# Rearranged transitions into and out of two FFN stages: one modulation vector moved to TensorE, other product order, other groups, a new cost in the order planner

## The chip, the cores and the metric

The kernel runs on one core of a Trainium2 chip. The metric is the device time of one execution in microseconds, as the median of several runs. The engines that matter here are TensorE (PE in the profile; its weight loads are PEld), VectorE (DVE), ScalarE (ACT), GpSimd (POOL) and the DMA queues, of which SyncE (SP) issues nearly all loads of weights. The engines run side by side, each through its own queue in order, and wait for one another through semaphores.

## The reference

Two layers of a generator block on 512 latent tokens and 256 context tokens of width 1024. The last layer doesn't update the context.

```python
for l in range(DEPTH):                                   # DEPTH = 2
    mod  = c_act  @ w_mod[l] + b_mod[l]                  # six vectors sh1 sc1 g1 sh2 sc2 g2 for the latents
    modc = cc_act @ w_mod[l] + b_mod[l]                  # and six for the context
    px = (rmsnorm(x, norm1_g[l]) * (1.0 + sc1) + sh1) @ w_in[l] + b_in[l]
    ...                                                  # three head groups: mLSTM, gated MLP, convolution -> y_x
    x = x + g1 * (y_x @ w_out[l])
    x = x + g2 * swiglu(rmsnorm(x, norm2_g[l]) * (1.0 + sc2) + sh2, w_gu[l], w_down[l])
    ...                                                  # the same for the context, if not the last layer
return rmsnorm(x, final_g)

def swiglu(h, w_gu, w_down):
    gate, up = split(h @ w_gu, 2)                        # hidden width 2816 = 22 tiles of 128
    return (silu(gate) * up) @ w_down
```

The modulation vectors are numbered 0 to 5 in the order above: vector 5 of layer 0 is g2, the gate of its FFN; vector 1 of layer 1 is sc1, which the first norm of layer 1 needs.

## The kernel before

**Numbers.** All matrix products are of float32 data, each operand being split into a rounded part `hi` and a rest `lo`; a product is three matmuls (hi·hi, hi·lo, lo·hi: lines 528 to 530 in the plain products, 1887 to 1889 in the paired ones). Weights arrive in `raw` buffers (four of 512 KB); ACT copies them to `hi` (L374, L457) and DVE subtracts to get `lo` (L376, L334). The split buffers (`spl`, four) hold a whole plain weight tile each or, in the FFN's paired part, are cut into eight units.

**The order.** The program is written as many small generators ("threads") that ask for an engine with a cost, for an event or for a buffer. A planner (`Plan.run`) plays them against each other with these costs, always taking the request that can start earliest, then by priority (a lower number first), and in doing so emits every engine's instructions. So the costs in `PE(n)`, `DVE2(n)`, `ACT(n)` decide in which order each in-order queue holds its work; they do nothing at run time. A main list `steps` sets PE's order and `ORDER` follows it for the weights' loads. `spread(a, b)` mixes list b evenly into list a.

**Modulation vectors.** A vector can be made in two ways. `mod_steps` does it on PE: eight steps, each of four matmuls (L650) that read a raw weight buffer and free it. `modh_steps` does it on DVE: eight loads of 512 KB, and per load two or four multiply-adds (L724 the first, L727 the others), four where both token kinds need the vector; each half ends with a few matmuls on PE (L737). Before, vectors 2, 3, 4 of layer 0 are made on PE in its first stage, vector 5 of layer 0 and vector 1 of layer 1 on DVE in the second half of that stage (32 DVE instructions each), and vectors 0, 2, 3, 4, 5 of layer 1 on DVE during layer 0's FFN.

**The FFN.** Its first tiles of hidden units (`NPLAIN`, two per layer) are computed plainly: gate and up columns of eight contraction steps over all tokens. Each further tile j is a "pair": gate and up column together form a 2 x 2 block product, done with seven products instead of eight, each over half of the contraction (four steps of three matmuls) and half of the tokens (384 in layer 0, 256 in layer 1). Weight sums are made by DVE in the raw buffers (L420); the sums of the activations, the "T-forms", are made once per layer: L1781 to L1790 on DVE, L1794 the copy on ACT, L1796 the rest on DVE, for k = 0 to 3. The products s1, s2, s3 and a22 need a form, step k the form of k; a11, a12 and s4 read the activations directly. In PSUM bank A collects a11, s2, s3, a22 in turn, and `copy_out` copies A after a11, s2 and s3 (`x`, `x`, `d`, L1958); d gets C added (L1962) before s4 goes into C; bank B holds a12. `pair_out` then makes the hidden tile from x, d, A, B and C. Order in a pair before: a11, then a22 and s4 of the pair before, then s1, s2, a12, s3.

The down projection runs in groups of hidden tiles (`FFN_GROUPS`: start and count). A group's eight columns times two token halves are mixed into the pairs' steps after its tiles are there (`D_BLOCKS`); each half's result is added to `xT` by DVE (L2023). The last group comes after the last pair, followed by the next norm (squares L778, sums L781, `stat` L831, the power on POOL L264, `rstdb` L846, then L893, L868, L870).

Of the kernel before, what the change touches and what calls it, by code (L numbers as in the profile page):

```python
# [31 lines left out]
RV_BV, RV_BVS, RV_BGT, RV_LG, RV_LB = 0, 512, 768, 784, 1040  # L32
NRV = 1296
WB_Q, WB_K, WB_O, WB_U, WB_A, WB_G = 0, 4, 8, 12, 14, 16
FFN_GROUPS = (((0, 4), (4, 4), (8, 4), (12, 4), (16, 3), (19, 3)), ((0, 6), (6, 6), (12, 5), (17, 5)))
NPLAIN = (2, 2)
D_BLOCKS = (2, 4)
PAIR = ("a11", "a22", "s4", "s1", "s2", "a12", "s3")
GV_SLABS = ((0, 3), (3, 3), (6, 2))


# [133 lines left out]


def PE(n, passes=1):
    return ("e", "pe", max(107.0, n / 2.4) * passes)


def MM(n):
# [42 lines left out]
def backbone(ctx, tc, xT_d, cT_d, wmod_d, wb_d, wgv_d, wv_d, wout_d, wgu_d, wd_d, sw_d, sb_d, cv_d, rv_d, id_d, mk_d, out_d):  # L224
    nc = tc.nc
    pe, dve, act, pool, sp = nc.tensor, nc.vector, nc.scalar, nc.gpsimd, nc.sync
# [46 lines left out]
    def ev(*key):  # L273
        if key not in EV:
            EV[key] = Event()
        return EV[key]
# [27 lines left out]
    def loader():  # L304
        for i, key in enumerate(ORDER):
            if key[0] == "x":
                yield DMA(P * T * 8)
                sp.dma_start(out=xT[:, key[1]:key[1] + 2, :], in_=xT_d[:, key[1]:key[1] + 2, :])
                fire(ev("x", key[1]), DMA_LAT)
                continue  # L310
            if key[0] == "gp":
                if key[3] == PAIR[0]:
                    RAW[key[:3]] = rs = []
                    for up in range(2):
                        yield A("raw")
                        r = buf("raw", [P, KD, P], "raw")
                        yield DMA(P * KD * P * 4)
                        sp.dma_start(out=r.rearrange("p a b -> p (a b)"), in_=wgu_d[key[1], 2 * key[2] + up])
                        rs.append(r)
                        fire(ev("raw", key[:3], up), DMA_LAT)  # L320
                continue
            src, a, b = wsrc(key)
            tag = "slot" if key[0] == "modq" else "raw"
            yield A(tag)
            r = buf(tag, [P, a, b], "raw")
            RAW[i] = r
            yield DMA(P * a * b * 4)
            sp.dma_start(out=r if key[0][:3] == "mod" else r.rearrange("p a b -> p (a b)"), in_=src)
            fire(ev("raw", i), DMA_LAT)
# [130 lines left out]
    def splitter():  # L460
        in_units = set()
        for i, key in enumerate(ORDER):
            if key[0] == "x":
                continue
            if key[0] == "gp":
                if key[1] not in in_units:
                    in_units.add(key[1])
                    spawn(to_units(), 6)
                yield A("un")
                SPL[i] = UN.pop(0)  # L470
                fire(ev("u", i))
                if key[3] == PAIR[0]:
                    spawn(pair_sums(key[:3]), 0)
                continue
            if key[0] == "d":
                if key[2] < len(FFN_GROUPS[key[1]]) - 1:
                    m = (wsrc(key)[1] + 3) // 4
                    yield A("un", m)
                    spawn(split_units(i, key, [UN.pop(0) for _ in range(m)]), 0)
                    continue  # L480
                if key[1] in in_units:
                    in_units.remove(key[1])
                    spawn(from_units(), 6)
            if key[0][:3] == "mod":
                spawn(as_is(i), 0)
                continue
            yield A("spl")
            spawn(split(i, key), 0)
# [424 lines left out]
    def spread(a, b):  # L913
        out, j = [], 0
        for i, x in enumerate(a):
            out.append(x)
            while j < len(b) and j * len(a) < (i + 1) * len(b):
                out.append(b[j])
                j += 1
        return out  # L920

    def layer(l):
        last = l == L - 1
# [12 lines left out]
        def E(*key):  # L936
            return ev(l, *key)
# [9 lines left out]
        steps = []  # L947
# [728 lines left out]
        mid = None  # L1676
        if l == 0:
            mid = True
        steps += tiles([k_col(h) for h in range(H)], GB, GA, KD, hsrc, hwait, wide=True, mid=mid, ahead=AHEAD[0])
        first = len(steps)  # L1680
# [7 lines left out]
        if not last:  # L1688
            steps = steps[:first] + spread(steps[first:], [m for v in (2, 3, 4) for m in mod_steps(l, v)])
# [16 lines left out]
        def out_col(d):  # L1706
            def evac(p, grp):
                yield from resid(l, 2, p, d, grp, lambda g: norm(l, 1, g))
            return (("o", l, d), evac, 0.5)

        def spawn_gs(m, which):
            def fn():
                spawn(norm_gs(m, which))
                return
                yield
            return ([], fn)

        steps.append(spawn_gs(l, 1))
        steps += tiles([out_col(d) for d in range(KD)], gl, gg, KD, hsrc, lambda k, g: E("ys", g["t0"], k), YK, wide=True, ahead=AHEAD[1])


        hid, gups = {}, {}
# [3 lines left out]
        fg = FFN_GROUPS[l]  # L1726
# [97 lines left out]
        def gu_col(i):  # L1824
            j, up = divmod(i, 2)

            def evac(p, g):
                if up:
                    yield from gu_evac(j, g, gups.pop((j, g["t0"])), p)
                else:  # L1830
                    gups[j, g["t0"]] = p
            return (("gu", l, i), evac, 0.6)
# [59 lines left out]
        def pair_steps(j, before):  # L1892
            key = ("gp", l, j)
            q = pr[j] = {}

            def first(w):
                yield A("ps")
                q["A"] = ps("bA")
                yield from product(q["A"], w, (0, 0), True)
                spawn(copy_out(j, 0), 0.6)  # L1900

            def fifth(w):
                yield A("ps")
                q["C"] = ps("bC")
                yield from product(q["C"], w, 0, True)

            def sixth(w):
                yield W(E("cp", j, 0))
                yield from product(q["A"], w, 3, False)
                spawn(copy_out(j, 1), 0.6)  # L1910

            def second(w):
                yield A("ps")
                q["B"] = ps("bB")
                yield from product(q["B"], w, (1, 0), True)
                spawn(join_one(j), 0.6)

            def seventh(w):
                yield W(E("cp", j, 1))
                yield from product(q["A"], w, 1, False)  # L1920
                spawn(copy_out(j, 2), 0.6)

            out = [([key + ("a11",)], first)]
            if before is not None:
                out += pair_end(before)
            return out + [([key + ("s1",)], fifth), ([key + ("s2",)], sixth), ([key + ("a12",)], second), ([key + ("s3",)], seventh)]

        def pair_end(j):
            q = pr[j]

            def fourth(w):
                yield W(E("cp", j, 2))
                yield from product(q["A"], w, 2, False)

            def third(w):
                yield W(E("join", j))
                yield from product(q["C"], w, (1, 1), False)
                spawn(pair_out(j), 0.5)
            return [([("gp", l, j, "a22")], fourth), ([("gp", l, j, "s4")], third)]
# [133 lines left out]
            return  # L2073
            yield

        if not last:
            early = [m for v in (5,) for m in modh_steps(l, v)] + modh_steps(l + 1, 1)
            late = first + (len(steps) - first) // 2
            steps = steps[:late] + spread(steps[late:], early)
        steps.append(([], lambda: spawn_ffn()))  # L2080
        np_ = NPLAIN[l]
        steps += tiles([gu_col(i) for i in range(2 * np_)], gl, gg, KD, hsrc, lambda k, g: ev("h", l, 1, g["t0"], k), wide=True, ahead=AHEAD[2])
        steps.append(([], plain_done))
        nfirst = len(steps)
        pairs = list(range(np_, NJ))
        blocks = [pair_steps(j, j - 1 if i else None) for i, j in enumerate(pairs)]
        for gi, (j0, nj) in enumerate(fg[:-1]):
            b0, ds = j0 + nj - np_ + 1, d_run(gi)
            nb = min(D_BLOCKS[l], len(blocks) - b0)
            for b in range(nb):  # L2090
                part = ds[b * len(ds) // nb:(b + 1) * len(ds) // nb]
                cut = 3 if blocks[b0 + b][1][0] else 1
                blocks[b0 + b] = blocks[b0 + b][:cut] + spread(blocks[b0 + b][cut:], part)
        for b in blocks:
            steps += b
        steps += pair_end(pairs[-1])
        if not last:
            steps = steps[:nfirst] + spread(steps[nfirst:], [m for v in (0, 2, 3, 4, 5) for m in modh_steps(l + 1, v, "wi")])
            steps.append(spawn_gs(l + 1, 0))
        steps.append(([], t_free))  # L2100
        steps += d_run(len(fg) - 1)
# [58 lines left out]
    for c in EARLY_LOADS + "m" * len(pkeys) + "w" * len(mkeys):  # L2160
        n = len(ORDER)
# [93 lines left out]
```

## Time and profile before

| | before |
|---|---|
| median of 3 runs | 1580.05 us (1579.65 to 1580.49) |
| profiled execution, its time | 1579.2 us |
| its span | 1577.4 us |
| mean granted PE clock | 0.982 |
| ACT busy | 678.1 us |
| weight DMA (q1) | 170.16 MB |

A span is the time from the first to the last instruction of the profiled execution. "Busy" rows of matmuls overlap, as matmuls are pipelined: the rate of PE is read from the distance between starts, not from the duration of one. A number in brackets at a row's end is the engine's idle time just before, with the instruction that ended it. "PEclk" is the share of the full clock that PE was granted.

### The profile page before, as it was taken

The numbers are of one execution on the slowest core, as the hardware profiler recorded it, in microseconds if no ns is written. First come the engines' busy times: TensorE is split into PE (matmuls) and PEld (weight loads), VectorE is DVE, ScalarE is ACT, GpSimd is POOL, SyncE is SP. The second block draws the span as 40 slices with busy tenths as digits, with TensorE's granted clock in tenths as the row PEclk, the third lists the DMA queues.
The fourth block names the chain that finished last, engine by engine and source line by source line (L and its number), as shares of the span: only waits on it lengthen the run. The fifth ranks groups of instructions, "written<-read, shape, count | busy, mean of one in ns | idle before, by whom it ended". The sixth has DMA issues, their size and how long they took to land.

```text
span 1577.4 us, 26171 instructions
## 1 busy us (share of the span) xinstructions
PE 1502.8 (95%) x10232; PEld 1398.8 (89%) x10232; DVE 1147.4 (73%) x2416; ACT 678.1 (43%) x1402; POOL 33.3 (2%) x50
## 2 busy tenths in 40 slices
PE   5999999999789999999999989999999799999997
PEld 4887888888689999999999988878999699999997
DVE  5359889777977876767777774687768876777765
ACT  4332367543433343333333343426655444444444
POOL 0000010000000000000000000000000000000000
PEclk9999999999989999999999989999999899999999
DMA  9433346543023334333334232213321223333331
GB/s 327 144 121 120 116 132 203 157 139 107 27 70 111 101 106 135 108 107 121 112 102 127 86 97 74 87 55 114 101 94 55 80 85 104 101 94 101 104 101 64
DMA packets 72824, 173.25 MB, mean 110 GB/s; under 512 B 7564, under 2 KB 20988, under 8 KB 72700
## 3 DMA queue, kind: packets, MB, share of 16 engines
q1 hardware_dynamic: 69932, 170.16, 34.1%
q8 instruction: 80, 1.31, 0.3%
q10 hardware_dynamic: 2768, 1.42, 0.3%
q14 instruction: 44, 0.36, 0.1%
HBM read 169.34 MB, written 2.21 MB: 109 GB/s over the span
## 4 chain that ended last, share of the span: by engine, by line
PE 90%; DVE 5%; DMA 2%; ACT 1%; issue 1%; POOL 0%; SPq 0%; POOLq 0%; DVEq 0%; ACTq 0%
PE mm L528 15%; PE mm L529 15%; PE mm L530 15%; PE bA L1887 6%; PE bA L1888 6%; PE bA L1889 6%; PE bC L1887 3%; PE bC L1888 3%; PE bC L1889 3%; PE vp L1304 2%; PE vp L1305 1%; PE vp L1306 1%; PE bB L1887 1%; PE bB L1889 1%; PE bB L1888 1%; PE stp L1441 1%
## 5 line engine op out<-in xcount | busy, mean ns | idle before, releaser
L528 PE MATMUL mm<-HH,hi 128*128 128x256 f32 (+2 forms) x1008 | 342.3, 340 | 2.9 <-ACT HH L1603 1.7
L529 PE MATMUL mm<-HH,hi 128*128 128x256 f32 (+2 forms) x1008 | 329.3, 327 | 2.6 <-DVE HH L870 2.3
L530 PE MATMUL mm<-HH,lo 128*128 128x256 f32 (+2 forms) x1008 | 329.0, 326 | 0.9 <-DVE lo L334 0.9
L374 ACT CAST hi<-raw 128x512 fp32r<-128x512 f32 (+3 forms) x368 | 214.5, 603 | 215.1 <-PE mm L529 47.5
L376 DVE TENSOR_TENSOR lo<-raw,hi 128x512 fp32r<-128x512 f32 (+3 forms) x368 | 236.7, 663 | 67.1 <-ACT hi L374 64.4
L528 PEld LDWEIGHTS mm<-HH,hi 128*128 128x128 f32 x1008 | 191.6, 190 | 24.0 <-issue 8.0
L530 PEld LDWEIGHTS mm<-HH,lo 128*128 128x128 f32 x1008 | 191.4, 190 | 16.2 <-DVE lo L334 1.3
L529 PEld LDWEIGHTS mm<-HH,hi 128*128 128x128 f32 x1008 | 191.9, 190 | 14.9 <-DVE HH L870 3.3
L530 PE MATMUL mm<-ffn,lo 128*128 128x256 f32 (+1 forms) x576 | 176.3, 306 | 2.1 <-DVE lo L376 2.1
L528 PE MATMUL mm<-ffn,hi 128*128 128x256 f32 (+1 forms) x576 | 177.1, 307 | 0.7 <-ACT ffn L2006 0.5
L529 PE MATMUL mm<-ffn,hi 128*128 128x256 f32 (+1 forms) x576 | 176.5, 306 | 0.5 <-DVE ffn L2001 0.3
L1888 PE MATMUL bA<-ffn,hi 128*128 128x384 f32 (+1 forms) x480 | 149.2, 311 | 0.0
L334 DVE TENSOR_TENSOR lo<-raw,hi 128x1024 fp32r<-128x1024 f32 (+4 forms) x90 | 99.0, 1104 | 68.2 <-ACT hi L457 62.8
L2023 DVE SCALAR_TENSOR_TENSOR xT<-mm,modc,xT 128x256 f32<-128x256 f32 (+2 forms) x208 | 95.4, 480 | 68.4 <-PE mm L530 67.2
L457 ACT CAST hi<-raw 128x1024 fp32r<-128x1024 f32 (+4 forms) x90 | 85.3, 952 | 132.2 <-PE mm L529 49.8
L420 DVE TENSOR_TENSOR raw<-raw 128x512 f32<-128x512 f32 x160 | 109.1, 686 | 19.3 <-DMA raw<-in_wgu 18.3
L1889 PE MATMUL bA<-HH,lo 128*128 128x256 f32 (+1 forms) x400 | 116.9, 292 | 0.0
L1887 PE MATMUL bA<-HH,hi 128*128 128x256 f32 (+1 forms) x400 | 116.9, 292 | 0.0
L530 PEld LDWEIGHTS mm<-ffn,lo 128*128 128x128 f32 x576 | 108.8, 189 | 2.4 <-DVE lo L376 2.4
L528 PEld LDWEIGHTS mm<-ffn,hi 128*128 128x128 f32 x576 | 108.5, 188 | 2.3 <-ACT ffn L2006 0.8
L529 PEld LDWEIGHTS mm<-ffn,hi 128*128 128x128 f32 x576 | 108.4, 188 | 1.0 <-DVE ffn L2001 0.5
L727 DVE SCALAR_TENSOR_TENSOR macc<-raw,csil,macc 128x512 f32<-128x512 f32 x140 | 102.5, 744 | 0.4
(263 smaller groups left out, 3010.2 us busy)
## 6 DMA issues: line engine op xcount, KB each, us to landing
raw<-in_wmod SPq DMA_DIRECT2D x96, 512.0 KB, 4.2
raw<-in_wgu SPq DMA_DIRECT2D x88, 512.0 KB, 4.0
raw<-in_wb SPq DMA_DIRECT2D x36, 512.0 KB, 3.6
pbt<-dr SPq DMA_DIRECT2D x40, 256.0 KB, 3.7
raw<-in_wout SPq DMA_DIRECT2D x16, 512.0 KB, 3.6
raw<-in_wd SPq DMA_DIRECT2D x32, 256.0 KB, 2.6
raw<-in_wd SPq DMA_DIRECT2D x16, 384.0 KB, 3.1
raw<-in_wd SPq DMA_DIRECT2D x16, 320.0 KB, 3.1
```

Source lines behind the costliest of these rows:

```text
L334: dve.tensor_tensor(lo, r, hi.bitcast(F32), ALU.subtract)
L374: act.copy(hi, x)
L376: dve.tensor_tensor(lo, x, hi.bitcast(F32), ALU.subtract)
L420: dve.tensor_tensor(o, x, y, op)
L528: pe.matmul(o, lhsT=hi[:, k, :], rhs=hh, start=(j == 0), stop=False)
L529: pe.matmul(o, lhsT=hi[:, k, :], rhs=hl, start=False, stop=False)
L530: pe.matmul(o, lhsT=lo[:, k, :], rhs=hh, start=False, stop=(j == nk - 1))
L727: dve.scalar_tensor_tensor(a[g], s[:, i, :], c, a[g], ALU.mult, ALU.add)
L1887: pe.matmul(o, lhsT=hi[:, k], rhs=rh, start=start and k == 0, stop=False, skip_group_check=True)
L1888: pe.matmul(o, lhsT=hi[:, k], rhs=rl, start=False, stop=False, skip_group_check=True)
L1889: pe.matmul(o, lhsT=lo[:, k], rhs=rh, start=False, stop=k == 3, skip_group_check=True)
L2023: dve.scalar_tensor_tensor(x, p[:, a - h["t0"]:b - h["t0"]], MODC[l][:, 5, d, g["g"]:g["g"] + 1], x, ALU.mult, ALU.add)
```

## The change

- `mod_steps(0, 5)`: vector 5 of layer 0 is made on PE, its eight steps spread from the middle of the out-projection (`nout`) to the end of the plain FFN columns. Vector 1 of layer 1 is made on DVE during layer 0's FFN, ahead of the others there.
- Pair order: a11, a22 and s4 of the pair before, s2, a12, s1, s3. The first pair of a layer: a11, a12, s2, s1, s3.
- `FFN_GROUPS`, layer 0: the last two groups have two and four tiles instead of three and three. `D_LAST`: the last eight steps of the last group but one come after the last pair, in both layers.
- `NPLAIN`: three plain tiles in layer 1.
- The planner's cost of a matmul: from n/2.4 to 1 + 0.455 n ns (at least 107). This lays out the order of all queues anew, over the whole kernel.

```diff
-FFN_GROUPS = (((0, 4), (4, 4), (8, 4), (12, 4), (16, 3), (19, 3)), ((0, 6), (6, 6), (12, 5), (17, 5)))
-NPLAIN = (2, 2)
+FFN_GROUPS = (((0, 4), (4, 4), (8, 4), (12, 4), (16, 2), (18, 4)), ((0, 6), (6, 6), (12, 5), (17, 5)))
+NPLAIN = (2, 3)
 D_BLOCKS = (2, 4)
-PAIR = ("a11", "a22", "s4", "s1", "s2", "a12", "s3")
+D_LAST = 8
...
 def PE(n, passes=1):
-    return ("e", "pe", max(107.0, n / 2.4) * passes)
+    return ("e", "pe", max(107.0, 1 + 0.455 * n) * passes)
...
+        nout = len(steps)
         steps += tiles([out_col(d) for d in range(KD)], gl, gg, KD, hsrc, lambda k, g: E("ys", g["t0"], k), YK, wide=True, ahead=AHEAD[1])
+        nout = (nout + len(steps)) // 2
...
             out = [([key + ("a11",)], first)]
+            mid = [([key + ("s2",)], sixth), ([key + ("a12",)], second)]
             if before is not None:
                 out += pair_end(before)
-            return out + [([key + ("s1",)], fifth), ([key + ("s2",)], sixth), ([key + ("a12",)], second), ([key + ("s3",)], seventh)]
+            else:
+                mid = mid[::-1]
+            return out + mid + [([key + ("s1",)], fifth), ([key + ("s3",)], seventh)]
...
-        if not last:
-            early = [m for v in (5,) for m in modh_steps(l, v)] + modh_steps(l + 1, 1)
-            late = first + (len(steps) - first) // 2
-            steps = steps[:late] + spread(steps[late:], early)
         steps.append(([], lambda: spawn_ffn()))
         np_ = NPLAIN[l]
         steps += tiles([gu_col(i) for i in range(2 * np_)], gl, gg, KD, hsrc, lambda k, g: ev("h", l, 1, g["t0"], k), wide=True, ahead=AHEAD[2])
+        if not last:
+            steps = steps[:nout] + spread(steps[nout:], mod_steps(0, 5))
...
             nb = min(D_BLOCKS[l], len(blocks) - b0)
+            if gi == len(fg) - 2:
+                ds, rest = ds[:-D_LAST], ds[-D_LAST:]
...
-        steps += pair_end(pairs[-1])
+        steps += pair_end(pairs[-1]) + rest
         if not last:
-            steps = steps[:nfirst] + spread(steps[nfirst:], [m for v in (0, 2, 3, 4, 5) for m in modh_steps(l + 1, v, "wi")])
+            steps = steps[:nfirst] + spread(steps[nfirst:], [m for v in (1, 0, 2, 3, 4, 5) for m in modh_steps(l + 1, v, "wi")])
```

More of the change, by code (lines that the diff above doesn't have):

```diff
@@ L311, in loader @@
             if key[0] == "gp":
-                if key[3] == PAIR[0]:
+                if key[3] == "a11":
                     RAW[key[:3]] = rs = []
@@ L471, in splitter @@
                 fire(ev("u", i))
-                if key[3] == PAIR[0]:
+                if key[3] == "a11":
                     spawn(pair_sums(key[:3]), 0)
```

## The prediction

> **What bounds the kernel now.** I read the page first (shares and span), then the 100 us windows to see which stages lose TensorE time, then TensorE's waits by releaser, and last the timelines inside the three worst stages.
>
> ```profile
> span 1577.4 us, 26171 instructions
> PE 1502.8 (95%) x10232; PEld 1398.8 (89%) x10232; DVE 1147.4 (73%) x2416; ACT 678.1 (43%) x1402; POOL 33.3 (2%) x50
> ```
>
> TensorE (PE) is busy 1502.8 of 1577.4 us, so 74.6 us of idle PE, plus stretches at a lower granted clock, is all that an order can win. The windows (columns: PE, PEld, DVE, ACT, POOL busy, then PE clock and DMA) show where it lies:
>
> ```profile
> 200.00:300.00 100.00, 98.37 (x739) 84.24 (x740) 82.54 (x256) 66.07 (x200) 11.61 (x15) 1.00 0.54 169
> 300.00:400.00 100.00, 99.01 (x634) 86.76 (x627) 75.14 (x138) 43.29 (x77) 2.15 (x2) 1.00 0.40 121
> 400.00:500.00 100.00, 83.03 (x425) 75.54 (x424) 81.78 (x132) 39.08 (x69) 0.00 (x0) 0.90 0.20 61
> 500.00:600.00 100.00, 99.67 (x591) 98.37 (x590) 76.31 (x137) 36.11 (x70) 0.00 (x0) 1.00 0.37 116
> 1200.00:1300.00 100.00, 85.77 (x691) 84.06 (x690) 84.43 (x163) 52.19 (x100) 0.70 (x1) 0.93 0.21 66
> ```
>
> The two bad windows are the entries into the two FFN stages (layer 0 near 420 us, layer 1 near 1220 us); inside the FFN (500 to 600) PE is full. The waits of PE name what ended them:
>
> ```profile
> PE bC L1888 <- DVE ffn L1796: 10.8, 5, 3.5
> PE bC L1887 <- ACT ffn L1794: 7.7, 3, 4.0
> PE bC L1887 <- DVE d L1962: 6.6, 4, 1.6
> PE bC L1887 <- ACT HH L1794: 4.9, 1, 4.9
> PE bA L1887 <- ACT x L1958: 1.6, 4, 0.6
> ```
>
> Lines 1794 and 1796 end the T-forms (10.8 + 7.7 + 4.9 = 23.4 us): the first pair's s1 product stands waiting while VectorE (DVE) makes them. Line 1962 is the sum d that s4 needs.
>
> **The change, part by part.**
>
> *1. Vector 5 of layer 0 to PE, vector 1 of layer 1 into the FFN.*
>
> ```profile
> 200.00:390.00 190.00, 40.50 (x56) 1.00 0.48 150
> 277.15 0.57 PE modps L650 x8
> 298.88 0.57 PE modps L737 x16
> ```
>
> The first row is line 727 alone (DVE's accumulation): 40.5 us in 56 instructions leave 200 to 390 us. With them go four PE steps like the L737 row, 4 x 0.57 = 2.3 us. In come eight steps like the L650 row, 8 x 0.57 = 4.6 us, spread over fourteen steps: four fall in the second half of the out-projection (2.3 us, which cancels the 2.3), four among the plain gate/up products, ahead of the T-form wait, where they cost nothing: the wait hides them, and would cost 2.3 us without it. PE is idle 1.6 + 1.0 = 2.6 us from 200 to 400; with less DVE work and 16 raw loads fewer there (8 come back) I take half: **-1.3** (0 to -2.6). Vector 1's two closing steps now stand in the full FFN: 2 x 0.57 = **+1.1** (up to +3 if its 32 DVE instructions delay a weight split; DVE has 24% free in the 500 row, and 22 us over 480 us are 5%). Queues: SP's eight loads of 512 KB for vector 5 stand ahead of the first pair's weights and hold up to two of the four raw buffers until PE reaches them; behind them wait those weights, split only when a unit comes free at the end of the plain products, so I cost this at nothing.
>
> *2. a12 before the T-forms (layer 0).* Rows of PE, with the idle time before each in brackets:
>
> ```profile
> 420.94 0.34 PE L1887 MATMUL bA<-HH,hi 128*128 128x384 f32 x1
> 422.84 0.34 PE L1889 MATMUL bA<-HH,lo 128*128 128x384 f32 x1
> 438.98 0.69 PE L1887 MATMUL bC<-ffn,hi 128*128 128x384 f32 x1 [4.03 <-ACT ffn L1794]
> 441.47 0.69 PE L1888 MATMUL bC<-ffn,hi 128*128 128x384 f32 x1 [1.80 <-DVE ffn L1796]
> 449.59 0.34 PE L1887 MATMUL bA<-HH,hi 128*128 128x384 f32 x1
> 430.00:440.00 10.00, 2.38 (x4) 1.07 (x4) 10.00 (x17) 3.14 (x6) 0.00 (x0) 0.50 0.00 0
> ```
>
> a11 issues 12 products with 11 steps in 1.90 us, 0.173 each, so a product of the pair is 2.1 us. The pair needs 60 x 0.173 = 10.4 us and takes 449.6 - 420.9 = 28.7: 18.3 us lost, until DVE, saturated (10.00 in the last row), finishes the fourth form at 441.5. The change leaves DVE's work there as it is, since line 727 hardly runs in it; it only moves a12 (which needs no form) in front of the wait. What is late next is still the fourth form. So **-2.1**, one product. Bounds: 0 if DVE splits a12 for it and the forms come later by as much; -6 if the new order lets the forms pass pair weights.
>
> *3. The order within a later pair.* s3 follows a12 and s1 instead of a12 alone, so the copy x that it needs has two products of cover. The 1.6 us of waits on x (L1958) mostly go: **-1.2** (0 to -1.6). The s4 product still comes two products after s3, as before; a22 keeps one product of cover.
>
> *4. Group ends.* (16,3),(19,3) become (16,2),(18,4) in layer 0: the same products and as many evictions. In both layers eight steps of the group before are kept for after the last pair, 8 x 6 x 0.173 = 8.3 us of PE in layer 0, over the end of the last hidden tile. There PE loses 0.66:
>
> ```profile
> 900.00:910.00 10.00, 9.34 (x52) 8.78 (x52) 5.55 (x13) 3.77 (x8) 0.00 (x0) 1.00 0.13 39
> 930.19 0.33 PE L530 MATMUL mm<-ffn,lo 128*128 128x384 f32 x1
> 933.69 1.01 PE L831 MATMUL stat<-onesD,acc 128*128 128x1 f32 x4 [3.17 <-DVE acc L781]
> 936.18 1.22 PE L846 MATMUL rstdb<-ident,rs 128*128 128x128 f32 x4 [1.48 <-POOL rs L264]
> 938.52 0.58 PE L528 MATMUL mm<-HH,hi 128*128 128x256 f32 x1 [1.11 <-ACT HH L868]
> 940.00:950.00 10.00, 10.00 (x63) 10.00 (x63) 7.49 (x18) 4.24 (x8) 1.18 (x1) 0.69 0.01 2
> ```
>
> **-0.7**. At the change of layers the context's last column is followed by three lag columns, which cover its norm: 3 x 9 x 0.173 = 4.7 us now, 3 x 12 x 0.173 = 6.2 us with groups of four. The wait of 3.17 shrinks by 1.6, and DVE's backlog of L781 sums, spread over 33 instead of 25 us, a little more: **-2.0** (0 to -6, the three waits together).
>
> *5. A third plain tile in layer 1.*
>
> ```profile
> 1221.52 0.28 PE L1887 MATMUL bA<-HH,hi 128*128 128x256 f32 x1
> 1222.82 0.28 PE L1889 MATMUL bA<-HH,lo 128*128 128x256 f32 x1
> 1232.72 0.58 PE L1887 MATMUL bC<-HH,hi 128*128 128x256 f32 x1 [4.90 <-ACT HH L1794]
> 1241.88 0.28 PE L1887 MATMUL bA<-HH,hi 128*128 128x256 f32 x1
> 1232.85 2.35 DVE L1796 TENSOR_TENSOR ffn<-tf,HH 128x1024 fp32r<-128x1024 f32 x2
> 1194.32 1.22 DVE L334 TENSOR_TENSOR lo<-raw,hi 128x1024 fp32r<-128x1024 f32 x1
> 1214.32 0.41 DVE L1859 TENSOR_TENSOR s<-s,mm 128x256 f32<-128x256 f32 x1
> 1220.00:1230.00 10.00, 4.37 (x33) 3.86 (x31) 10.00 (x16) 2.51 (x5) 0.00 (x0) 0.81 0.33 106
> ```
>
> Here 11 steps take 1.30 us, 0.118 each; 60 products are 7.1 us, and 1221.5 to 1241.9 is 20.4: 13.3 us lost. A plain tile is 2 x 8 x 3 x 2 = 96 products of 256 columns, a pair 7 x 4 x 3 = 84: 12 more, +1.4 us. But it puts 96 x 0.118 = 11.3 us of PE work, and a12 1.4 more, in front of the wait. PE then meets the first form near 1235, when the last forms were done already in the old order (1232.85 + 2.35); and the pair weights, which DVE split between the forms, come later, since their buffers come free with the plain tiles. The extra tile's two splits and four eviction steps cost DVE 2 x 1.22 + 4 x 0.41 = 4.1 us. I leave 1.4 us of the wait: -13.3 + 1.4 + 1.4 = **-10.5** (-4 to -12).
>
> *6. The planner's PE cost.* It was n/2.4 = 107 ns for 256 columns and becomes 1 + 0.455 x 256 = 117; the rows above measure 118. It alone sets the order on every queue. In layer 1 the old plan gave a pair 84 x 107 = 9.0 us of PE against 9.0 us of DVE by its own costs (eleven sums and splits of 0.6, six small steps), so DVE looked full and weight splits (priority 0) went ahead of the sum d (0.6):
>
> ```profile
> 1251.94 0.37 ACT L1958 COPY d<-bA 128x256 f32<-128x256 f32 x1 [0.89 <-PE bA L1889]
> 1255.91 0.41 DVE L1962 TENSOR_TENSOR d<-d,bC 128x256 f32<-128x256 f32 x1
> 1256.37 0.39 PE L1887 MATMUL bC<-HH,hi 128*128 128x256 f32 x1 [1.65 <-DVE d L1962]
> 1260.00:1270.00 10.00, 8.35 (x71) 8.14 (x70) 7.58 (x15) 4.59 (x11) 0.00 (x0) 1.00 0.17 50
> ```
>
> d's copy is done at 1252.3 and its sum starts 3.6 us later, behind splits; PE waits 1.65 us in each such pair. With 84 x 117 = 9.9 us of PE in the plan DVE has room, and d goes ahead; there is also one pair fewer. Of the 6.6 us I take three of four waits: **-4.9** (0 to -6.6). Elsewhere the new order moves instructions that the trace can't show; I take nothing, bounded by one such 1.65 us per pair (rival 3).
>
> Sum: -1.3 + 1.1 - 2.1 - 1.2 - 0.7 - 2.0 - 10.5 - 4.9 = -21.6 us. The profiled execution took 1579.2 us, so 1557.6; the median of the three runs is 0.85 above it, which gives **1558 us**.
>
> The clock: PE restarts at 0.69 after waits of 3.17, 1.48 and 1.11 us, and stays at 1.00 through lone waits of 1.65. The Trainium skill ("TensorE: Matmul & The Clock Gate", Part 1, the HAM clock gate) says that the clock halves after an idle window of about 3.4 us and comes back after as long a busy one. Read by single waits it would not have halved at the layer change, so here the trace differs, and decides; what the rule would give is rival 5.
>
> **The rivals.**
> 1. *The forms stay late in layer 1.* DVE is saturated there and gets 4 us more; if the forms end at 1239 and not 1235, PE waits 4 us and cools for some 2 more. Against it: the pair weights come later. -21.6 + 6 = about 1564; with d's waits kept too, 1569.
> 2. *The forms come earlier in layer 0*, past the pair weights, by some 4 us, and d's waits all go: 1552.
> 3. *Slower.* The new order starves one sum in the full FFN of layer 0 as d was starved: 1.65 us in each of 20 pairs, +33, so 1591. It decides from 13 pairs on (21.6 / 1.65). For it: DVE gets 5% more there; against: 76% busy, PE at 99.67.
> 4. *It does nothing*: the fourth form and d's sum are late as before by the same amount, as DVE is full ahead of both: 1579.
> 5. *The clock stays full at the layer change*, since the waits there get shorter: (1 - 0.69) x 10 = 3.1 us more, 1555. That is the rule of the skill's page named above, read by single waits.
>
> **How the numbers follow.** Forecast (1552 to 1564) 0.50; rival 1 0.20; rival 2 0.16; rival 5 0.05; rival 3 0.06; rival 4 0.03. What can be told from no change is 0.2%, 3 us. Slower is rival 3, the same is rival 4: faster 0.91, same 0.03, slower 0.06. From 1558 down, the unused bounds of parts 1, 2, 5 and 6 (1.3 + 3.9 + 1.4 + 1.7) and 3.1 of clock reach 1546; up, rival 1 with d's waits and part 2 gone (6 + 4.9 + 2.1) reaches 1571.
>
> **What would show it.** Right: no line 727 before 400 us and a fourth group of L650 near 380 to 420; the wait at the first pair of layer 0 still on L1794 and L1796, some 4 us shorter; the 1220 to 1250 windows of layer 1 at clock 1.00 with little idle; no wait on L1962; the gap before the first product of layer 1 near 6 us. Wrong: L1796 still ending waits in layer 1, or new waits on x, d or a weight split in every pair.

## The result and the profile after

The changed kernel takes 1557.45 us (median, 1556.11 to 1559.97) against 1580.27 us for the kernel before on the same chip: 0.9857 of it, interval 0.9840 to 0.9874, a gain of 22.8 us. The forecast was 1558. The total came out; several terms did not, and that their errors cancel is luck. The profiled execution took 1559.97 us, the slowest of its four, with a span 19.3 us below that of before.

The page of the changed kernel, span and engines:

```profile
span 1558.1 us, 26164 instructions
PE 1503.7 (97%) x10276; PEld 1396.0 (90%) x10276; DVE 1119.8 (72%) x2372; ACT 675.1 (43%) x1395; POOL 32.9 (2%) x50
```

PE's busy time rose by 0.9 us while the span fell by 19.3, so the gain shows as idle time. (Products were added, but a low clock stretches busy time, and the granted clock rose from 0.982 to 0.990.) The 100 us windows (columns as in the prediction: PE, PEld, DVE, ACT, POOL, clock, DMA):

```profile
100.00:200.00 100.00, 97.80 (x589) 76.53 (x589) 92.86 (x235) 32.87 (x63) 5.01 (x9) 0.98 0.31 104
200.00:300.00 100.00, 96.31 (x704) 82.90 (x704) 61.55 (x217) 63.72 (x198) 8.41 (x12) 1.00 0.43 137
400.00:500.00 100.00, 92.64 (x513) 84.69 (x512) 91.30 (x150) 45.46 (x80) 0.00 (x0) 0.95 0.25 80
1200.00:1300.00 100.00, 96.69 (x817) 96.24 (x815) 87.54 (x167) 54.38 (x106) 0.00 (x0) 1.00 0.25 80
```

Both FFN entries are better: PE 83.03 to 92.64 at 400, and 85.77 to 96.69 at 1200, where the clock went from 0.93 to 1.00. But 200 to 300, where PE had stood still for 1.6 us only, fell from 98.37 to 96.31. PE's waits by releaser say the same:

```profile
PE bA L1889 <- ACT x L1963: 6.9, 4, 3.1
PE mm L529 <- DVE HH L870: 4.3, 3, 2.6
PE bA L1890 <- DVE ffn L1798: 3.3, 2, 2.8
PE hT L1565 <- DVE hacc L1560: 3.0, 2, 1.6
```

(Lines 1794, 1796, 1958 and 1962 of before are 1796, 1798, 1963 and 1967 here.) The forms end 3.3 us of waits where they ended 23.4, and none on the sum d is left (1.1 us on its copy are). The copy x, which ended 1.6 us, now ends 6.9, most of it at the first pairs; new is `hT`, a product of the head groups, at 223 and 251 us. PE at the first pair of layer 0 and of layer 1:

```profile
395.72 1.05 PE L831 MATMUL stat<-onesD,acc 128*128 128x1 f32 x8
429.80 0.34 PE L1889 MATMUL bA<-HH,hi 128*128 128x384 f32 x1
436.09 0.44 PE L1889 MATMUL bA<-ffn,hi 128*128 128x384 f32 x1 [1.96 <-ACT x L1963]
442.15 0.69 PE L1890 MATMUL bA<-ffn,hi 128*128 128x384 f32 x1 [2.80 <-DVE ffn L1798]
448.08 0.34 PE L1889 MATMUL bA<-HH,hi 128*128 128x384 f32 x1
1229.10 0.28 PE L1889 MATMUL bA<-HH,hi 128*128 128x256 f32 x1
1235.21 0.39 PE L1889 MATMUL bA<-HH,hi 128*128 128x256 f32 x1 [3.13 <-ACT x L1963]
```

The first row, the norm's statistics ahead of the FFN, stood at 390.46 before:

```profile
390.46 0.95 PE L831 MATMUL stat<-onesD,acc 128*128 128x1 f32 x8
```

With such landmarks each execution can be cut into six stretches that add up to its span: A to that `stat`; B on to the second pair's a11; C to the last product of the down projection of layer 0; D to the first gv product (L977) of layer 1; M to the `stat` ahead of layer 1's FFN; E to the end. The last two columns are what the clock took from A and from D, as one minus the granted clock, times the length. In us, one profiled execution each (the runs e1 to e12 are told below):

| | A | B | C | D | M | E | span | clock lost in A | in D |
|---|---|---|---|---|---|---|---|---|---|
| before | 390.5 | 59.1 | 480.6 | 47.4 | 222.5 | 377.3 | 1577.4 | 0 | 6.8 |
| after | 395.7 | 52.4 | 484.1 | 41.3 | 222.7 | 361.9 | 1558.1 | 3.4 | 3.4 |
| e5 (after again) | 389.8 | 53.4 | 483.5 | 42.6 | 222.7 | 361.6 | 1553.6 | 0 | 5.1 |
| e1 new cost alone | 393.2 | 54.9 | 477.1 | 45.6 | 223.1 | 373.9 | 1567.9 | 0 | 5.1 |
| e2 all but the cost | 387.6 | 56.8 | 481.1 | 39.7 | 222.5 | 374.9 | 1562.7 | 1.7 | 1.7 |
| e3 two plain tiles | 392.9 | 53.8 | 481.4 | 39.8 | 221.7 | 369.6 | 1559.3 | 3.4 | 1.7 |
| e4 old pair order | 391.6 | 54.7 | 483.9 | 41.4 | 222.6 | 367.3 | 1561.6 | 1.7 | 3.4 |
| e6 vectors as before | 394.8 | 55.5 | 479.0 | 38.3 | 222.9 | 363.8 | 1554.2 | 1.7 | 0 |
| e7 groups as before | 391.5 | 52.6 | 481.4 | 46.2 | 222.8 | 363.3 | 1557.9 | 0 | 5.1 |
| e8 new cost from the FFN on | 387.2 | 49.3 | 482.3 | 42.6 | 223.2 | 363.0 | 1547.7 | 0 | 5.1 |
| e9 e8, vector 1 early | 389.2 | 52.3 | 475.1 | 41.3 | 223.6 | 363.9 | 1545.3 | 1.7 | 3.4 |
| e10 e8, both vectors early | 389.9 | 56.5 | 475.3 | 41.4 | 223.1 | 362.2 | 1548.4 | 0 | 3.4 |
| e11 e8, evictions first | 388.3 | 59.4 | 480.5 | 42.5 | 221.8 | 365.0 | 1557.4 | 1.7 | 5.1 |
| e12 e8, three plain tiles twice | 385.8 | 61.8 | 468.9 | 41.4 | 223.2 | 362.4 | 1543.6 | 0 | 3.4 |

After and e5 are one program: A differs by 5.9 us between them, so a few us in A of a single execution say little; B, C and E repeat within 1 us. Of the 5.9, 3.4 are clock: after had a clock of 0.98 in the windows from 0 and from 100 us, e5 of 1.00. The rest, 2.5, is idle time of PE (24.4 us in A of after, 21.8 in e5). The first window of after, then of e5:

```profile
0.00:100.00 100.00, 81.53 (x697) 68.86 (x698) 41.07 (x91) 35.07 (x58) 1.92 (x6) 0.98 0.62 208
```

```profile
0.00:100.00 100.00, 81.39 (x703) 68.97 (x704) 41.51 (x92) 36.41 (x60) 1.92 (x6) 1.00 0.63 213
```

Two borders need care. With the new groups the context's `stat` and `rstdb` come ahead of the down projection's last product and count in C; with the old groups they come after it and count in D. So C and D are best added. In e12 a plain tile stands in B and one pair fewer in C.

### The profile page after: what moved, and what is told of

The parts are those of the page before. It is cut to its first block, busy times and chain, and to the rows that moved or that the text cites. A ratio compares the mean times of both kernels' runs of the same rounds, so it can differ in the third digit from the quotient of the medians.

```text
span 1558.1 us, 26164 instructions
## 1 busy us (share of the span) xinstructions
PE 1503.7 (97%) x10276; PEld 1396.0 (90%) x10276; DVE 1119.8 (72%) x2372; ACT 675.1 (43%) x1395; POOL 32.9 (2%) x50
## 4 chain that ended last, share of the span: by engine, by line
PE 73%; DVE 16%; DMA 6%; issue 3%; ACT 2%; POOL 0%; SPq 0%; POOLq 0%; DVEq 0%; ACTq 0%
PE mm L528 13%; PE mm L529 13%; PE mm L530 13%; PE bA L1889 4%; PE bA L1890 4%; PE bA L1891 4%; DVE lo L376 3%; DMA raw<-in_wgu 2%; PE bC L1889 2%; PE bC L1890 2%; PE bC L1891 2%; DMA raw<-in_wd 2%; DVE macc L727 2%; DVE raw L420 1%; PE vp L1304 1%
## 5 line engine op out<-in xcount | busy, mean ns | idle before, releaser
L528 PE MATMUL mm<-HH,hi 128*128 128x256 f32 (+2 forms) x1040 | 351.3, 338 | 0.3 <-ACT HH L1603 0.3
L529 PE MATMUL mm<-HH,hi 128*128 128x256 f32 (+2 forms) x1040 | 338.1, 325 | 5.4 <-DVE HH L870 4.3
L530 PE MATMUL mm<-HH,lo 128*128 128x256 f32 (+2 forms) x1040 | 337.8, 325 | 0.2 <-DVE lo L334 0.2
L374 ACT CAST hi<-raw 128x512 fp32r<-128x512 f32 (+2 forms) x361 | 209.8, 599 | 251.0 <-PE mm L529 59.6
L376 DVE TENSOR_TENSOR lo<-raw,hi 128x512 fp32r<-128x512 f32 (+2 forms) x361 | 228.6, 658 | 30.2 <-ACT hi L374 27.2
L528 PEld LDWEIGHTS mm<-HH,hi 128*128 128x128 f32 x1040 | 197.4, 190 | 23.6 <-issue 10.7
L529 PEld LDWEIGHTS mm<-HH,hi 128*128 128x128 f32 x1040 | 197.9, 190 | 17.7 <-DVE HH L870 5.2
L530 PEld LDWEIGHTS mm<-HH,lo 128*128 128x128 f32 x1040 | 197.1, 190 | 15.3 <-DVE lo L334 0.4
L420 DVE TENSOR_TENSOR raw<-raw 128x512 f32<-128x512 f32 x156 | 103.6, 685 | 27.0 <-DMA raw<-in_wgu 25.8
L1889 PE MATMUL bA<-HH,hi 128*128 128x256 f32 (+1 forms) x384 | 112.2, 292 | 3.6 <-ACT x L1963 3.1
L1891 PE MATMUL bA<-HH,lo 128*128 128x256 f32 (+1 forms) x384 | 112.0, 292 | 0.0
L1890 PEld LDWEIGHTS bA<-ffn,hi 128*128 128x128 f32 x468 | 88.1, 188 | 4.1 <-DVE ffn L1798 4.1
```

What stands on the lines that cost most here:

```text
L374: act.copy(hi, x)
L376: dve.tensor_tensor(lo, x, hi.bitcast(F32), ALU.subtract)
L420: dve.tensor_tensor(o, x, y, op)
L528: pe.matmul(o, lhsT=hi[:, k, :], rhs=hh, start=(j == 0), stop=False)
L529: pe.matmul(o, lhsT=hi[:, k, :], rhs=hl, start=False, stop=False)
L530: pe.matmul(o, lhsT=lo[:, k, :], rhs=hh, start=False, stop=(j == nk - 1))
```

## The experiments

The theory carried over from the prediction: each edit acts in its own stretch. The rivals are that the new cost alone does it, or that parts of the change lose what others win. e1 to e4 ran on one chip, e5 to e8 and e12 on a second, e9 to e11 on a third; every ratio is against the kernel before on the same chip, and kernels of different chips are compared by their ratios.

**e1: the new cost alone, on the kernel before.**

```diff
-    return ("e", "pe", max(107.0, n / 2.4) * passes)
+    return ("e", "pe", max(107.0, 1 + 0.455 * n) * passes)
```

> The kernel before with the planner's new PE cost (1 + 0.455 n) and nothing else. Theory A (the new order is behind the end of the waits on d, behind the earlier T-forms of layer 0 and behind the losses ahead of both FFNs): no wait on L1962 in layer 1 (-5 to -7 us), T-forms of layer 0 some 4 us earlier, but the first 395 us longer by about 5 and layer 1's mixer by 2; in all 1572 to 1580. Theory B (the structural edits did it all, the cost hardly matters): 1579 to 1581, waits on L1962 still 6.6 us and the first norm statistics of the latents at 390.5 us as before.

Measured: 1571.01 us, 0.9937 (0.9924 to 0.9949). 9.7 us of the gain need no other edit. E fell by 3.4 only, B by 4.2, C by 3.5. The waits on d are halved, not gone:

```profile
PE bC L1887 <- DVE d L1962: 3.7, 4, 0.9
```

**e2: everything but the new cost.**

```diff
-    return ("e", "pe", max(107.0, 1 + 0.455 * n) * passes)
+    return ("e", "pe", max(107.0, n / 2.4) * passes)
```

> The changed kernel with the old PE cost (n/2.4). Theory A: the waits on d come back in layer 1 (+5 to +7), the T-forms of layer 0 end later (+4), and the first 395 us are shorter by some 5, layer 1's mixer by 2: 1557 to 1563. Theory B: no wait on d, as the pair order removed it, and 1556 to 1559 with the same losses ahead of the FFNs.

Measured: 1564.94 us, 0.9896 (0.9881 to 0.9911). The gains of e1 and e2, 9.7 and 15.7 us, add up to 25.4, a little more than the whole change gives. With the old cost A is 387.6 for 390.5 before, but d still stops PE, in fewer and longer waits:

```profile
PE bC L1889 <- DVE d L1967: 5.9, 3, 2.3
```

**e3: two plain tiles in layer 1.**

```diff
-NPLAIN = (2, 3)
+NPLAIN = (2, 2)
```

> The changed kernel with two plain tiles in layer 1, as before. Theory A (the third plain tile covers the T-forms): the wait on L1794 and L1796 in layer 1 returns, about 11 us net: 1566 to 1570. Rival (the new order and a12 ahead cover most of it): 2 to 4 us slower, or faster by the 1.4 us of extra products: 1556 to 1562.

Measured: 1561.44 us, 0.9879 (0.9866 to 0.9893) for 0.9857 of after. In E the third tile is worth 369.6 - 361.9 = 7.7 us, in the total by these ratios some 3.5 (the intervals overlap). Between the two profiles stretches A to M, the same program there, took back 6.6 us: 1189.6 in e3 and 1196.2 in after. The 1561.44 us lie in the range of the rival, not of theory A. The forms stop PE in layer 1 again:

```profile
PE bA L1890 <- DVE ffn L1798: 6.9, 4, 2.8
PE bA L1889 <- ACT HH L1796: 4.9, 1, 4.9
```

**e4: the old order of products in a pair.**

```diff
-            return out + mid + [([key + ("s1",)], fifth), ([key + ("s3",)], seventh)]
+            return out + [([key + ("s1",)], fifth), ([key + ("s2",)], sixth), ([key + ("a12",)], second), ([key + ("s3",)], seventh)]
```

> The changed kernel with the old order of products in all pairs (a11, a22 and s4 of the pair before, s1, s2, a12, s3). Theory A (the order gives one product of cover ahead of the forms and a longer cover for the copies x): +3 to +5 us: 1560 to 1563, no wait on d. Rival (the order is what ended the waits on d): waits on L1962 back, +7 to +12: 1564 to 1570.

Measured: 1565.13 us, 0.9902 (0.9888 to 0.9915) for 0.9857 (0.9840 to 0.9874) of after: the new order is worth 0.45%, some 7 us (against e5, the same kernel measured again, 0.31% or 5 us, and there the intervals just overlap). Here too the total is in the range of the rival. B loses 2.3 us, E 5.4, and d is back:

```profile
PE bC L1889 <- DVE d L1964: 3.5, 4, 0.9
```

So it takes both edits to end the waits on d: the cost alone (e1) leaves 3.7 us, the whole change without the cost (e2) 5.9 and without the order (e4) 3.5, both together none.

**e5: the changed kernel again**, unchanged, on the second chip.

> The changed kernel itself once more, to see how far its stages move between executions: layer 0 up to its last norm statistics took 1196.2 us in its first profile and 1189.7 in that of the kernel with two plain tiles, whose instructions there are the same. If that is chance of the execution: 1555 to 1559, and a layer 0 between 1189 and 1196. If the first profile shows the kernel's own layer 0, 1196 again.

Measured: 1559.36 us (1555.43 to 1563.11), 0.9871 (0.9850 to 0.9891). Single executions of this program spread by 7.7 us, more than most of the terms under dispute. Layer 0 up to its last statistics took 1192.0 us, for 1196.2 in after, so much of that first profile was chance.

**e6: both vectors as before**, 5 of layer 0 and 1 of layer 1 on DVE ahead of the FFN.

```diff
+            early = [m for v in (5,) for m in modh_steps(l, v)] + modh_steps(l + 1, 1)
+            late = first + (len(steps) - first) // 2
+            steps = steps[:late] + spread(steps[late:], early)
...
-            steps = steps[:nout] + spread(steps[nout:], mod_steps(0, 5))
...
-            steps = steps[:nfirst] + spread(steps[nfirst:], [m for v in (1, 0, 2, 3, 4, 5) for m in modh_steps(l + 1, v, "wi")])
+            steps = steps[:nfirst] + spread(steps[nfirst:], [m for v in (0, 2, 3, 4, 5) for m in modh_steps(l + 1, v, "wi")])
```

> The changed kernel with vector 5 of layer 0 and vector 1 of layer 1 made on DVE ahead of the FFN, as before. Theory A (the move frees DVE and raw buffers ahead of the FFN and hides half of its PE time in the wait for the T-forms): 2 to 4 us slower, the first norm statistics of the latents later than in the changed kernel by 1 to 3. Rival (its 4.6 us of PE on a full PE are worth more than DVE's time): 1 to 3 us faster, with statistics at 391 or earlier.

Measured: 1554.82 us, 0.9837 (0.9822 to 0.9852): undoing this part is not slower; its median is 4.5 us below that of e5, though the intervals touch and that of after's own measurement (0.9840 to 0.9874) overlaps, so a gain is not shown either. B is 2.1 to 3.1 us longer, as the relief of DVE would have it, but C is 4.5 to 5.1 shorter and D 3.0 to 4.3. D's part is the clock: nothing lost here, 3.4 and 5.1 in after and e5. The theory that taking the 40 us off DVE ahead of the FFN pays 2 to 4 us fell, under this order.

**e7: the groups as before, no steps kept back.**

```diff
-(16, 2), (18, 4)), ...
+(16, 3), (19, 3)), ...
-            if gi == len(fg) - 2:
-                ds, rest = ds[:-D_LAST], ds[-D_LAST:]
...
-        steps += pair_end(pairs[-1]) + rest
+        steps += pair_end(pairs[-1])
```

> The changed kernel with the old groups of layer 0 (three and three) and no eight steps kept for after the last pair. Theory A: the change of layers loses its cover: 3 to 6 us slower, most of it between the last pair of layer 0 and the first products of layer 1 (before: a gap of 8.2 us), under 1 us at the end of layer 1. Rival (the new cost alone brings the norm's sums in time): 0 to 1 us.

Measured: 1559.84 us, 0.9874 (0.9861 to 0.9888), not to be told from e5, as the rival had it. D is 46.2, near the 47.4 of before, and 42.6 in e5, which lost as much clock there: 3.6 us for the edit. But C is 2.1 shorter without it than in e5, in part because `stat` and `rstdb` of the context moved from C to D. Together C and D take 527.6 us for 526.1: 1.5 us are won. The waits that the longer cover removes come back in the profile of e7:

```profile
PE rstdb L846 <- POOL rs L264: 3.6, 2, 2.5
PE stat L831 <- DVE acc L781: 3.5, 3, 2.0
```

**e8: the new cost only from layer 0's FFN on.** All that stands before is planned with the old cost.

```diff
+IN_FFN = [False]
...
-    return ("e", "pe", max(107.0, 1 + 0.455 * n) * passes)
+    return ("e", "pe", max(107.0, 1 + 0.455 * n if IN_FFN[0] else n / 2.4) * passes)
```

(`spawn_ffn` of layer 0 sets it.)

> The changed kernel with the old PE cost up to the start of layer 0's FFN and the new one from there on. Theory A (the new cost loses some 4 to 5 us in the first stage through its order alone and wins in the FFNs): 1551 to 1554, statistics of the latents at 387 to 389 us and no wait on d. Rival (the loss ahead of the FFN comes with the moved vector, or later stages take it back): 1556 to 1559.

Measured: 1548.74 us, 0.9800 (0.9782 to 0.9817), against 0.9871 (0.9850 to 0.9891) for e5 on the same chip. The intervals don't touch: planned with the more exact cost ahead of the FFN, the kernel is slower. The first stage shows it in every execution: less the clock lost, A is 385.8 to 387.2 with the old cost there (e2, e8, e11, e12) and 389.5 to 392.3 with the new (after, e3, e4, e5, e7). Those 2.3 to 6.5 us are not all of it: between the two profiles, which differ by 5.9 us of span, A has 2.6 and B 4.1. The windows of e8 and of e5 over the first stage:

```profile
100.00:200.00 100.00, 100.00 (x607) 78.35 (x606) 90.55 (x230) 31.31 (x59) 3.22 (x6) 1.00 0.36 114
200.00:300.00 100.00, 98.84 (x729) 85.91 (x728) 65.43 (x224) 67.23 (x201) 11.04 (x15) 1.00 0.45 136
```

```profile
100.00:200.00 100.00, 98.08 (x604) 77.02 (x604) 92.60 (x234) 34.60 (x66) 5.00 (x9) 1.00 0.34 107
200.00:300.00 100.00, 98.69 (x713) 84.38 (x711) 63.32 (x218) 62.81 (x195) 8.39 (x12) 1.00 0.44 140
```

e8 loses 1.2 us of PE in the two windows, e5 3.2 and after 5.9. What was lost are small waits in the head groups (`glast`, `cT`, `mixp`, of 0.3 to 0.8 us in e5's first stage, and in the profile of after 3.0 us of `hT`, for 1.2 in both e5 and e8), not one wait that repeats. B gains as well, 49.3 against 53.4, nearly all at the first pair (15.6 for 19.3 us). There the clock was 1.00 in e8 and 0.73 in e5; PE's longest wait is 2.3 us in e8 and 2.7 in e5.

**e9: e8, with vector 1 of layer 1 on DVE ahead of the FFN.**

```diff
+            late = first + (nout - first) // 2
+            steps = steps[:late] + spread(steps[late:nout], modh_steps(l + 1, 1)) + steps[nout:]
...
-            steps = steps[:nfirst] + spread(steps[nfirst:], [m for v in (1, 0, 2, 3, 4, 5) for m in modh_steps(l + 1, v, "wi")])
+            steps = steps[:nfirst] + spread(steps[nfirst:], [m for v in (0, 2, 3, 4, 5) for m in modh_steps(l + 1, v, "wi")])
```

> The changed kernel with the old PE cost ahead of layer 0's FFN, and with vector 1 of layer 1 made on DVE in the second half of the first stage again, spread up to the middle of the out-projection; vector 5 stays on PE. Theory A (vector 1 costs the FFN of layer 0 3 to 4 us where the changed kernel has it): 2 to 4 us faster than the kernel with the late cost alone (1548.7), so 1545 to 1547, the FFN from the second pair to its last product 479 us instead of 482. Rival (DVE and raw buffers ahead of the FFN are worth as much): 1548 to 1550.

Measured: 1548.44 us, 0.9798 (0.9783 to 0.9812): the same as e8. C is 7.2 us shorter without the vector, A and B are 2.0 and 3.0 longer with it there. Where the vector stands moves time between stretches and wins nothing.

**e10: e8, with both vectors on DVE early** (e6's edit on e8).

```diff
+            early = [m for v in (5,) for m in modh_steps(l, v)] + modh_steps(l + 1, 1)
...
-            steps = steps[:nout] + spread(steps[nout:], mod_steps(0, 5))
```

> The same late cost with both vectors on DVE ahead of the FFN, as before. Theory A (vector 5 on PE costs nothing, since half of it lies in the wait for the T-forms): 1 to 3 us slower than with vector 5 on PE, so 1547 to 1550. Rival (4.6 us on PE cost more than DVE's time, as the kernel with both vectors on DVE was 4.5 us faster than the changed kernel): 1543 to 1546.

Measured: 1550.77 us, 0.9817 (0.9802 to 0.9831). B is 56.5 against e9's 52.3: vector 5 on PE does help the first pair, in these two profiles. In the total that is 0.2%, or 2.3 us: all four executions of e10 (from 1550.01) lie above all four of e9 (up to 1549.57), but the intervals overlap, so this part stays unproven.

**e11: e8, with the evictions of the plain tiles ahead of weight splits.**

```diff
-            return (("gu", l, i), evac, 0.6)
+            return (("gu", l, i), evac, -0.1)
```

> The late cost, and the evictions of the plain gate and up columns ahead of the weight splits on DVE and ACT (priority -0.1 instead of 0.6). Theory C (the 3.1 us wait on the copy x at the first pair of layer 1, and 2 us in layer 0, stand behind an eviction that stands behind five splits): 3 to 5 us faster than 1548.7, that wait gone. Rival (the splits come later by as much and the first pair waits for weights): 1547 to 1552.

Measured: 1559.16 us, 0.9866 (0.9849 to 0.9882), some 10 us slower than e8 and beyond both expectations. The waits on the copy x did shrink, from 5.7 us to 1.4, but the forms came later, and B rose by 10.1:

```profile
PE bA L1894 <- ACT ffn L1801: 8.7, 2, 7.3
```

**e12: e8, with a third plain tile in layer 0 too.**

```diff
-NPLAIN = (2, 3)
+NPLAIN = (3, 3)
```

> The kernel with the late cost (1548.7) and three plain tiles in layer 0 too. Theory A (what a plain tile does in layer 1 it does in layer 0: PE gets 16.6 us more ahead of the T-forms for 12 products of 384 columns, 2.1 us, and the first pair, 15.6 us where 60 products need 10.4, loses its 5 us): 2 to 4 us faster, 1545 to 1547, no wait on the forms in layer 0. Rival (DVE is saturated there and the extra tile's splits and evictions push the forms back as far, or its hidden tile waits for its buffer): 1549 to 1553.

Measured: 1545.42 us (1544.68 to 1546.05), 0.9772 (0.9755 to 0.9788), the fastest of all, for 0.9871 (0.9850 to 0.9891) of the changed kernel on that chip. Its window at the entry into layer 0's FFN:

```profile
400.00:500.00 100.00, 100.00 (x576) 92.28 (x575) 87.08 (x146) 40.28 (x72) 0.00 (x0) 1.00 0.30 98
```

PE is never idle there, and the first pair takes 10.4 us, the bare 60 products. In e8 it took 15.6; 5.2 us saved less the plain tile's 12 extra products (12 x 0.173 = 2.1) is 3.1, and the medians differ by 3.3.

## Where the prediction was right and where wrong

By stretches (predicted, then after minus before): A -1.3, +5.3; B -2.1, -6.7; C and D +1.1 - 0.7 - 2.0 = -1.6, -2.6; M 0, +0.2; E -10.5 - 4.9 = -15.4, -15.4. The x term, -1.2, was to fall on B, C and E. Sum: -21.6 forecast, -19.3 between the two profiled executions, -22.8 between the medians. A's +5.3 against B's -6.7 is the largest pair of errors that cancel.

**Part 1 failed twice.** The failing step for A is the last sentence of part 6, "Elsewhere the new order moves instructions that the trace can't show; I take nothing": the bound put there looked into the full FFN (rival 3), not at the stage before it. The relief itself was real and larger than costed: with the old cost there and less the clock lost, A is 385.8 to 387.2, and 390.5 and 389.9 with both vectors on DVE (before, e10). The new cost took it back: 389.5 to 392.3 in the five executions that share this order. The size of the +5.3 is in part chance: 3.4 of it are clock, and in e5, the same program, A is 389.8 for the 390.5 of before. What else grew are the waits of DVE for the broadcasts `pbt<-dr`, 40 of 256 KB, which feed the head groups. The view of one tile, `pbt`, over the whole execution: the idle time (us, times) that its landing ended, nearly all of it DVE's, and the landing times; of before, of e8, of after, of e5 and of e1:

```profile
  DMA pbt<-dr: 10.5, 15
DMA to landing us min/median/max: 3.1/3.7/5.9
```

```profile
  DMA pbt<-dr: 11.1, 13
DMA to landing us min/median/max: 3.0/3.9/5.2
```

```profile
  DMA pbt<-dr: 19.9, 16
DMA to landing us min/median/max: 3.0/3.6/6.8
```

```profile
  DMA pbt<-dr: 20.0, 18
DMA to landing us min/median/max: 3.0/3.5/6.6
```

```profile
  DMA pbt<-dr: 14.4, 13
DMA to landing us min/median/max: 3.0/3.9/5.9
```

Under the new order DVE waits 9 us more for them, in e5 as in after, though the median broadcast is no slower; e2, with the old cost, has 12.7. But A does not follow them: e1 has 14.4 us of these waits and an A of 393.2, e5 20.0 and 389.8. PE waits at the end of a head group's chain, in after:

```profile
222.90 0.44 PE L1565 MATMUL hT<-ident,hacc 128*128 128x128 f32 x2 [1.31 <-DVE hacc L1560]
251.15 0.41 PE L1565 MATMUL hT<-ident,hacc 128*128 128x128 f32 x2 [1.64 <-DVE hacc L1560]
```

That the new order makes the stage longer is shown by e8. Through what it does so stays open: no run took the wait for the broadcasts alone away, and e1 speaks against it as the only cause. For C, "+1.1 (up to +3)" was the term mis-sized: vector 1 costs 7.2 us there under e8's order (482.3 against 475.1). PE's extra work is the 1.1. Its waits in that stretch are 4.4 us in e8 and 1.3 in e9, spread over a weight split (1.4), the copies x and d, and `macc`; what the remaining 3 us are was not found.

**Part 2: rival 2 happened, though not its total.** The forms came earlier, and d's waits went. From the `stat` to the last form's product it was 441.47 - 390.46 = 51.0 us before and is 442.15 - 395.72 = 46.4 after. Those 4.6 and a12's 2.1 are the 6.7 of stretch B. "What is late next is still the fourth form" holds (2.80), but "the change leaves DVE's work there as it is" does not hold, and the cost is why: from `stat` to the last form's product e1, the cost alone, takes 46.1 us, and e2, all but the cost, 50.2. So B splits into 4.2 by the cost (e1), for which nothing was put, and 2.3 by the rest (e2), which is the forecast 2.1.

**Part 3 was wrong.** Waits on x went from 1.6 to 6.9 us. At the first pair s2 now goes into the bank that x is copied from, with a12 alone between; 1.96 and 3.13 us of the 6.9 stand there, and 1.8 us are in two later pairs. The 1.96 in layer 0 need not cost anything, since the same product s2 then stands for the fourth form (2.80). In layer 1 it is a queue on ACT, fed by DVE. ACT of after, then DVE:

```profile
1234.40 0.41 ACT L1866 CAST ffn<-s 128x256 fp32r<-128x256 f32 x1 [1.72 <-DVE s L1861]
1234.79 0.37 ACT L1963 COPY x<-bA 128x256 f32<-128x256 f32 x1
```

```profile
1230.94 3.09 DVE L376 TENSOR_TENSOR lo<-raw,hi 128x512 fp32r<-128x512 f32 x5
1233.95 0.41 DVE L1861 TENSOR_TENSOR s<-s,mm 128x256 f32<-128x256 f32 x1
```

The copy stood behind a cast that waited for a plain tile's sum, which stood behind five weight splits.

**Part 4 held in sum only.** C and D together gave -2.6 for -1.6 forecast, by a gain of 6.1 in D against a loss of 3.5 in C. But 3.4 of the gain are clock (6.8 us lost in D before, 3.4 after), and e7 finds 1.5 us behind the group ends where 0.7 + 2.0 were forecast. What is late next at the change is `HH` of L870, 2.62 us.

**Parts 5 and 6 held in sum, one short and one beyond.** The first pair of layer 1 takes 10.5 us against 7.1 of products, so 3.4 us are lost where 1.4 were left, and by x rather than by a form: -13.3 + 3.4 + 1.4 = -8.5 (e3: 7.7) for -10.5. The waits on d went wholly, -6.6 for -4.9. Together -15.1 of the -15.4 seen. That the cost alone sets d ahead was half of it: it needed part 3's order (e1, e4).

**Rival 5, the clock.** The rival had the clock stay full there; that happened in one execution of those with the new groups, e6. The layer change of e5, then of e6: PE's wait, and 10 us after it (PEclk is the third column from the end).

```profile
929.78 0.58 PE L529 MATMUL mm<-HH,hi 128*128 128x256 f32 x1 [2.62 <-DVE HH L870]
930.00:940.00 10.00, 10.00 (x49) 10.00 (x50) 5.42 (x15) 3.05 (x6) 1.01 (x1) 0.52 0.19 54
```

```profile
932.30 0.38 PE L529 MATMUL mm<-HH,hi 128*128 128x256 f32 x1 [2.59 <-DVE HH L870]
932.00:942.00 10.00, 9.70 (x81) 9.67 (x82) 9.68 (x22) 5.72 (x11) 1.01 (x1) 1.00 0.20 54
```

A wait of the same length halves the clock in one execution (49 matmuls in 10 us) and leaves it full in the other (81). After and e5, one program, lost 3.4 and 5.1 us of clock in D after it. Ten executions have this single wait of some 2.6 us at the layer change (after, e3 to e6, e8 to e12); the table gives their losses in D, 0 to 5.1 us. Read by single waits, the rule of the Trainium skill ("TensorE: Matmul & The Clock Gate", Part 1) fails again, since 2.6 us is below its 3.4. The same section also says that the gate's window runs freely, so that the time at which the clock changes depends on where in it the first matmul falls; chance of that kind would fit these losses, and no run here tests it. D is 42.6 in e5 against 38.3 in e6: this toss is worth 4 us and more.

## What to carry to other kernels

A cost made more exact in a planner is a new order everywhere, not only where its error was seen: try it stage by stage, as e8 did (10.6 us faster in the median than the same cost throughout). Work put ahead of a wait of an in-order engine pays while its own price (2.1 us for the third plain tile in layer 0) stays below the wait that it covers (5.2); then ask which copy or eviction is late next, as x was here. And before terms of 1 to 3 us are believed, run the same program twice: here its executions differ by up to 7.7 us; and look at the granted clock of each stage before a difference is put down to an edit.

## What the runs showed of the hardware

After a wait of 2.6 us of PE the clock halved in nine executions of ten, and the time lost differed between executions of one program: 3.4 us in D of after, 5.1 of e5. Over all fourteen executions the losses in A and D come in steps of some 1.7 us (0, 1.7, 3.4, 5.1, 6.8). The 256 KB broadcast `pbt<-dr` lands after 3.6 us in the median of after and 3.9 of e8; its worst case was 6.8 and 5.2 us.
